# Inverting the delta rule's 64-row blocks: eight tiles in one pass, with the small blocks turned on the engines

## The chip, the cores and the metric

The kernel runs on one core of a Trainium2 chip. A core has five engines that run beside each other, each in the order of its own instructions: TensorE (PE in the profile; its weight loads, which overlap the matmuls, are PEld), VectorE (DVE), ScalarE (ACT), GpSimd (POOL) and SyncE (SP), which in this kernel issues almost all DMAs. The metric is the device time of one execution in microseconds (us); lower is better.

## What is computed

The reference is one layer of a streaming encoder over 1024 rows of 1024 channels. A combined projection feeds two branches: a gated DeltaNet with 8 heads, and a chunked attention with 16 heads. Both are projected, gated, merged, normalised, and followed by a feed-forward part with a short convolution. The change lies in the DeltaNet, in the solve of its chunked delta rule. Cut to what matters:

```
a_low = where(strict, (k_beta @ k^T) * decay, 0)          # per chunk of 64 rows
sol = triangular_solve(a_low + eye, rhs, lower=True, unit_diagonal=True)
u, w = sol[..., :dv], sol[..., dv:]
qk = where(causal, (q @ k^T) * decay, 0)
def step(state, inp):                                     # over the 16 chunks, in order
    v_new = u_n - w_n @ state
    o_n = (q_n * exp(g_n)) @ state + qk_n @ v_new
    state = state * exp(g_last) + k_dec^T @ v_new
```

The kernel works on tiles of 128 rows, so a head has eight tiles (two chunks of the reference each), and it forms the inverse of the unit lower triangular 128x128 matrix of each tile instead of solving.

## The kernel before, in words

The DeltaNet takes about the span's stretch from 80 to 930 us. A loop over the 8 heads `h` runs these stages, in program order: `stage_solve(h)`, `stage_inverse(h)`, some dense blocks of gates (`some_gates`), `stage_k(h+1)`, `stage_q(h+1)`, two pieces of another product (`mod_rows`), `stage_vz(h+1)`, `stage_chain(h)` and `stage_out(h)`. The order of the instructions on each engine is not the program order: a planner lays them out at build time by priorities and by its own estimate of every duration. `stage_inverse`, `stage_chain` and `stage_out` are put 2000 places ahead in priority, and `stage_k(h+1)` is held behind the last chain step of head `h-1` on each engine. Once laid out, an engine keeps its order: a TensorE instruction whose operand is late stops every later one on TensorE, dense work too.

What the stages around the change do, for one head:

- `stage_k` forms `am`, the eight 128x128 matrices (lines 596 to 605), and sends their 32x32 diagonal blocks through DRAM (`fa_d`, lines 606 to 614), so that `fa` holds each of the 32 blocks (4 blocks times 8 tiles) in a partition of its own.
- `stage_solve` inverts the 32 blocks at once by forward substitution on VectorE: 31 steps of one multiplication (line 670) and one reduction (line 672). A partition of `ft` holds 8 columns of one block's inverse. Then four DMAs write `ft` to DRAM (`ft_d`, line 674), and four more read it back (line 677) as diagonal blocks of the eight 128x128 matrices `dt_`, whose remaining entries were set to zero once.
- `stage_inverse` builds the inverse of the whole matrix from its diagonal blocks, in two groups `g` of four tiles. Each group has four waves of small matmuls on TensorE, all in the one PSUM bank of ring `i`, each followed by copies that the next wave needs: `pxt` (line 694), `py` (lines 706 to 708), `pzz` (line 714) and `pT` (line 720). Line 689 transposes 128x512 of `dt_` into `dd` for each group; lines 696, 697, 709 to 711, 716 and 721 empty the waves, and lines 698 to 703 and 717 fill and clear blocks of `am` on GpSimd.
- `stage_chain` goes through the tiles one after another, with matmuls on `am`, `kd`, `at` and the running state (lines 730 to 754). Its waits are TensorE to VectorE or ScalarE and back.

Dense matmuls of 128x128 by 128x512 (line 284 and, after the DeltaNet's middle, those of the attention, lines 891 and 906) stand between these small ones in TensorE's order. SP's order holds the weight loads (line 185) beside the DMAs of lines 674 and 677. POOL subtracts a rounded copy from each 128x1024 weight block (line 180), which takes 2412 ns in the mean.

Of the kernel before, what the change touches and what calls it, by code (L numbers as in the profile page):

```python
# [9 lines left out]
F32 = mybir.dt.float32  # L10
F32R = mybir.dt.float32r
AF = mybir.ActivationFunctionType
ALU = mybir.AluOpType
# [4 lines left out]
P = 128  # L18
# [3 lines left out]
NT = 8  # L22
# [37 lines left out]
_T, _E0, _E1 = ([f"{n}{i}" for i in range(m)] for n, m in (("T", 4), ("A", 7), ("B", 7)))  # L60


def _at(group, step_, n, first=0):
    return tuple((group, first + step_ * i) for i in range(n))
# [11 lines left out]
    "eg": _at("C", 0, 1, 656), "al": _at("C", 0, 1, 720), "dtb": _at("C", 0, 1, 728),  # L76
    "one": _at("C", 0, 1, 736),

    "tmp": tuple(_T), "dT": _at("G", 0, 1), "fa": _at("G", 0, 1, 1024), "dd": _at("G", 512, 2, 2048),
    "xt": _at("G", 256, 2, 3072), "zd": _at("G", 256, 2, 3584),  # L80
    "ft": _at("F", 256, 2), "pr": _at("F", 256, 2, 512), "gt": _at("GG", 512, 2),
    "vn": _at("V", 128, 3), "sn": _at("V", 128, 3, 384), "jk": _at("V", 0, 1, 768),
    **{n: (_E0[i], _E1[i]) for i, n in enumerate(("y0", "y1", "am", "at", "kd", "vs", "sz"))},
# [57 lines left out]
def hybrid_layer(  # L141
# [7 lines left out]
    PE, DVE, ACT, POOL, SP = nc.tensor, nc.vector, nc.scalar, nc.gpsimd, nc.sync  # L149
# [74 lines left out]
    def nm(s):  # L224
        uid[0] += 1
        return f"{s}_{uid[0]}"
# [7 lines left out]
    turn, groups = {}, {}  # L234
# [26 lines left out]
    def ring(key, shape, dtype=F32):  # L261
        return place(step(key, AT[key]), shape, dtype, key)
# [5 lines left out]
    def mtile(name, tag="m"):  # L268
        return pbank(name, tag)
# [156 lines left out]
    with tc.issue_after(mark0["x"]):  # L426
        o = VO["b_gate"]
# [65 lines left out]
    group("SM", "SM", 184)  # L493
    group("V", "SA", 1024)
    group("GG", "GT", 1024)
    dt_ = ring("dT", [P, NT, P])
    POOL.memset(dt_, 0.0)
    POOL.memset(groups["G"][:, 3072:4096], 0.0)
    B = [slice(32 * i, 32 * i + 32) for i in range(4)]

    def big(name):
# [2 lines left out]
    def flat(t_):  # L504
        return t_.rearrange("p t d -> p (t d)")

    def mbank(name, tag="m"):
        return mtile(nm(name), tag).rearrange("p (t d) -> p t d", t=4)
# [47 lines left out]
    def stage_k(h):  # L556

        c = {}
        gb = c["gb"] = big("gb")
        SP.dma_start(flat(gb),  # L560
                     gcum_d[h:h + 1, :].partition_broadcast(P).rearrange("p o s -> p (o s)"))
        mm = c["mm"] = big("mm")
        DVE.tensor_tensor(mm, gb, gc[:, h, :].unsqueeze(2).to_broadcast([P, NT, P]),
                          ALU.subtract)
        ACT.activation(flat(mm), flat(mm), AF.Abs)
        ACT.activation(flat(mm), flat(mm), AF.Exp, scale=-1.0)
        ACT.activation(flat(gb), flat(gb), AF.Exp)
        egl = c["egl"] = sm("egl")
        DVE.tensor_copy(egl, gb[:, :, P - 1])

        kT = c["kT"] = conv_in(h, 1)
        if h == 0:
            dump("kT", flat(kT))
        kd = c["kd"] = big("kd")
        ss = c["ss"] = sm("ss", 2 * NT)
        for g in range(2):
            pk = mbank("pk")
            for t in range(4):
                PE.transpose(pk[:, t, :], kT[:, 4 * g + t, :], ident)
            for t in range(4):  # L580
                u = 4 * g + t
                sumsq(ss[:, u:u + 1], pk[:, t, :])
            for t in range(4):
                u = 4 * g + t
                DVE.tensor_scalar(kd[:, u, :], pk[:, t, :], mm[:, u, P - 1:P], None, ALU.mult)
        kss = sm("kss")
        DVE.tensor_scalar(kss, ss[:, 0:NT], L2_EPS, None, ALU.add)
        rk = rsq(kss, "k")
        bk = c["bk"] = sm("bk")
        DVE.tensor_tensor(bk, rk, beta[:, h, :], ALU.mult)  # L590
        bkk = sm("bkk")
        DVE.tensor_tensor(bkk, bk, rk, ALU.mult)
        nbe = c["nbe"] = sm("nbe")
        DVE.scalar_tensor_tensor(nbe, bkk, -1.0, eg[:, h, :], ALU.mult, ALU.mult)

        am = c["am"] = big("am")
        for g in range(2):
            pk = mbank("pkk")
            for t in range(4):
                PE.matmul(pk[:, t, :], kT[:, 4 * g + t, :], kT[:, 4 * g + t, :],  # L600
                          start=True, stop=True)
            for t in range(4):
                u = 4 * g + t
                DVE.scalar_tensor_tensor(am[:, u, :], pk[:, t, :], bkk[:, u:u + 1],
                                         mm[:, u, :], ALU.mult, ALU.mult)
        fa_d = scr.tile([4, NT, 32, 32], F32, tag="fa_d", bufs=2, name=nm("fa_d"))
        c["ft_d"] = scr.tile([4, NT, 32, 32], F32, tag="ft_d", bufs=2, name=nm("ft_d"))
        for b in range(4):
            SP.dma_start(fa_d[b].rearrange("t i j -> i t j"),
                         am[32 * b:32 * b + 32, :, 32 * b:32 * b + 32])  # L610
        fa = c["fa"] = ring("fa", [P, 32, 32])
        for q in range(4):
            SP.dma_start(fa[32 * q:32 * q + 32].rearrange("p i j -> p (i j)"),
                         fa_d.rearrange("b t i j -> (b t) (i j)"))
        POOL.memset(fa.rearrange("p i j -> p (i j)")[:, 0:1024:33], -1.0)  # L615
        POOL.memset(am[0:64, :, 64:P], 0.0)
        POOL.tensor_tensor(mm, mm, tri.unsqueeze(1).to_broadcast([P, NT, P]), ALU.mult)
        return c
# [43 lines left out]

    def stage_solve(h, c):

        fa, ft_d = c["fa"], c["ft_d"]
        ft = ring("ft", [P, 8, 32])
        POOL.tensor_copy(ft, tt0)
        for i in range(1, 32):
            pr = ring("pr", [P, 8, 32])
            DVE.tensor_tensor(pr[:, :, 0:i + 1], ft[:, :, 0:i + 1],  # L670
                              fa[:, i:i + 1, 0:i + 1].to_broadcast([P, 8, i + 1]), ALU.mult)
            DVE.tensor_reduce(ft[:, :, i:i + 1], pr[:, :, 0:i + 1], AX.X, ALU.add, negate=True)
        for q in range(4):
            SP.dma_start(ft_d[:, :, 8 * q:8 * q + 8, :].rearrange("b t c j -> (b t) (c j)"),
                         ft[32 * q:32 * q + 32].rearrange("p c j -> p (c j)"))
        for b in range(4):
            SP.dma_start(dt_[32 * b:32 * b + 32, :, 32 * b:32 * b + 32],
                         ft_d[b].rearrange("t c j -> c t j"))

    def stage_inverse(h, c):  # L680


        am = c["am"]
        B0, B1, B2, B3 = B
        lo_, hi_ = slice(0, 64), slice(64, P)
        for g in range(2):
            G = slice(4 * g, 4 * g + 4)
            dd = ring("dd", [P, 4, P])
            DVE.transpose(flat(dd), flat(dt_)[:, 512 * g:512 * g + 512])
            px_ = mbank("pxt", "i")  # L690
            for t in range(4):
                u = 4 * g + t
                for i, j in ((B0, B1), (B2, B3)):
                    PE.matmul(px_[i, t, j], am[:, u, i], dt_[:, u, j], start=True, stop=True)
            xt = ring("xt", [P, 4, 64])
            ACT.activation(xt[B0, :, 0:32], px_[B0, :, B1], AF.Copy, scale=-1.0)
            DVE.tensor_scalar(xt[B2, :, 32:64], px_[B2, :, B3], -1.0, None, ALU.mult)
            for b in (B2, B3):
                POOL.tensor_copy(am[b, G, b], dt_[b, G, b])
            POOL.memset(am[B1, G, B0], 0.0)  # L700
            POOL.memset(am[B3, G, B2], 0.0)
            for b in (B0, B1):
                POOL.tensor_copy(am[b, G, b], dt_[b, G, b])
            py = mbank("py", "i")
            for t in range(4):
                PE.matmul(py[B2, t, B3], dd[:, t, B2], xt[:, t, 32:64], start=True, stop=True)
                PE.matmul(py[B0, t, B1], dd[:, t, B0], xt[:, t, 0:32], start=True, stop=True)
                PE.matmul(py[B1, t, B0], xt[:, t, 0:32], dd[:, t, B0], start=True, stop=True)
            DVE.tensor_copy(am[B2, G, B3], py[B2, :, B3])
            DVE.tensor_copy(dd[B1, :, B0], py[B1, :, B0])  # L710
            ACT.copy(am[B0, G, B1], py[B0, :, B1])
            pz = mbank("pzz", "i")
            for t in range(4):
                PE.matmul(pz[lo_, t, lo_], am[:, 4 * g + t, lo_], am[:, 4 * g + t, hi_], start=True, stop=True)
            zd = ring("zd", [P, 4, 64])
            ACT.activation(zd[lo_], pz[lo_, :, lo_], AF.Copy, scale=-1.0)
            POOL.memset(am[hi_, G, lo_], 0.0)
            pT = mbank("pT", "i")
            for t in range(4):
                PE.matmul(pT[lo_, t, lo_], dd[:, t, lo_], zd[:, t, :], start=True, stop=True)  # L720
            DVE.tensor_copy(am[lo_, G, hi_], pT[lo_, :, lo_])

    def stage_chain(h, c):

# [825 lines left out]
```

## Time and profile before

| | us |
|---|---|
| median of 3 runs | 2217.51 |
| lowest and highest of the 3 | 2213.31, 2221.87 |
| the profiled execution | 2222.63 |
| its span, first to last instruction | 2220.5 |

A row of the profile that groups instructions reads: line, engine, operation, result and operands by their names, out and in shapes, the count; then the busy time in us, the mean ns of one, and the idle time of that engine just before them with what ended it. A row of waits reads: who waited for whom, the sum in us, how many times, the longest. A row of windows gives a stretch, its length, and the busy time of PE, PEld, DVE, ACT and POOL in it with their instruction counts in brackets, then the TensorE clock that was granted as a share of full speed, the DMA share and GB/s. A row of the timeline gives the start, the duration, the instruction, and in square brackets the idle time before it.

### The profile page before, as it was taken

To read this page: it belongs to the slowest core of one execution; us is meant where nothing else is said; L and a number is where in the kernel's file an instruction comes from. 1 tells how busy PE (TensorE), PEld (TensorE's weight loads), DVE (VectorE), ACT (ScalarE), POOL (GpSimd) and SP (SyncE) were. 2 spreads that over 40 slices of the span, in tenths; PEclk is the share of its full clock that TensorE was granted. 3 is DMA by queue.
4 is the path that set the end of the run, shared out by engine and by line. 5 is a ranking of instruction groups with operands and counts; after the bars stand their busy time and mean duration, and the time that the engine had idled before them with its cause. 6 is when DMAs were issued, how large, how long until landed. Compare 5 with 4: busy or idle time off the path is not lost.

```text
span 2220.5 us, 31618 instructions
## 1 busy us (share of the span) xinstructions
PE 2140.7 (96%) x11577; PEld 1793.2 (81%) x11577; DVE 1477.9 (67%) x3096; ACT 999.6 (45%) x2127; POOL 500.9 (23%) x495
## 2 busy tenths in 40 slices
PE   7989999999999999999999899999999999999998
PEld 6778788777878787798989788888788888888886
DVE  6478476674758754567776653456998788875754
ACT  5634243443524334566765642234654444453331
POOL 0223233222323322233432422400120000000000
PEclk9999999999999999999999999999999999999999
DMA  9242323323243403211211424332232222275540
GB/s 289 86 121 71 113 80 106 110 74 110 78 120 87 128 24 99 68 51 50 72 55 60 148 96 128 114 128 95 76 102 70 78 83 86 90 260 210 171 152 38
DMA packets 227453, 232.01 MB, mean 104 GB/s; under 512 B 28058, under 2 KB 179027, under 8 KB 227299
## 3 DMA queue, kind: packets, MB, share of 16 engines
q1 hardware_dynamic: 227219, 229.98, 33.0%
q8 instruction: 91, 1.49, 0.3%
q14 instruction: 63, 0.52, 0.1%
q10 hardware_dynamic: 80, 0.03, 0.0%
HBM read 189.02 MB, written 47.23 MB: 106 GB/s over the span
## 4 chain that ended last, share of the span: by engine, by line
PE 49%; DVE 3%; ACT 1%; issue 1%; DMA 0%; POOL 0%; DVEq 0%; SPq 0%; ACTq 0%; POOLq 0%
PE pup L1268 17%; PE pdn L1422 11%; PE pbr L1049 8%; PE pwo L1110 4%; PE pqk L891 2%; PE pv L906 2%; PE po L981 2%; PE pp L966 1%; PE ps L940 1%; PE pn L1133 0%; DMA raw<-in_w_branch_a_dram 0%; DVE G L1329 0%; DVE t L170 0%; DVE kl L1011 0%; DVE pl L970 0%
## 5 line engine op out<-in xcount | busy, mean ns | idle before, releaser
L180 POOL TENSOR_TENSOR wl<-raw,wh 128x1024 fp32r<-128x1024 f32 x85 | 204.8, 2412 | 334.2 <-ACT wh L177 306.3
L1268 PE MATMUL pup<-hh,wop 128*128 128x512 f32 x704 | 224.2, 390 | 0.4 <-ACT G L1305 0.4
L1268 PE MATMUL pup<-t,wop 128*128 128x512 f32 x792 | 189.5, 392 | 1.4 <-DVE cc L1309 0.8
L1268 PEld LDWEIGHTS pup<-t,wop 128*128 128x128 f32 x792 | 148.6, 188 | 34.8 <-DVE cc L1309 1.2
L1422 PE MATMUL pdn<-dop,dop 128*128 128x512 f32 x696 | 161.6, 391 | 0.0
L177 ACT CAST wh<-raw 128x1024 fp32r<-128x1024 f32 x88 | 92.4, 1050 | 147.4 <-DMA raw<-in_w_in_dram 63.8
L1268 PEld LDWEIGHTS pup<-hh,wop 128*128 128x128 f32 x704 | 132.1, 188 | 29.1 <-ACT G L1305 0.8
L1422 PEld LDWEIGHTS pdn<-dop,dop 128*128 128x128 f32 x696 | 130.7, 188 | 28.3
L284 PE MATMUL pqkv<-hh,wh 128*128 128x512 f32 x352 | 142.8, 406 | 0.0
L284 PE MATMUL pqkv<-hl,wh 128*128 128x512 f32 x352 | 140.5, 399 | 0.0
L284 PE MATMUL pqkv<-hh,wl 128*128 128x512 f32 x352 | 140.2, 399 | 0.0
L1268 PE MATMUL pup<-hl,wop 128*128 128x512 f32 x352 | 137.2, 390 | 0.0
L670 DVE TENSOR_TENSOR FT<-FT,G 128x16 f32<-128x16 f32 (+30 forms) x248 | 121.6, 490 | 20.5 <-POOL G L615 13.1
L1310 POOL TENSOR_TENSOR cc<-cc,G 128x512 f32<-128x512 f32 x22 | 44.4, 2019 | 375.5 <-DVE G L1292 352.3
L951 POOL TENSOR_SCALAR G<-G,FT 128x640 f32<-128x640 f32 (+4 forms) x103 | 70.3, 685 | 182.4 <-DVE FT L950 161.6
L177 ACT CAST wop<-wr 128x512 fp32r<-128x512 f32 x104 | 61.9, 620 | 99.4 <-DVE wr L1250 66.9
L284 PE MATMUL pgt<-hh,wh 128*128 128x512 f32 x240 | 95.6, 399 | 0.4 <-DVE tmp L537 0.4
L284 PE MATMUL pgt<-hh,wl 128*128 128x512 f32 x240 | 94.7, 395 | 0.0
L284 PE MATMUL pgt<-hl,wh 128*128 128x512 f32 x240 | 94.7, 395 | 0.0
L180 DVE TENSOR_TENSOR wop<-wr,wop 128x512 fp32r<-128x512 f32 x104 | 75.3, 731 | 16.8 <-ACT wop L177 16.2
L970 DVE TENSOR_TENSOR pl<-pp,ph 128x512 fp32r<-128x512 f32 (+2 forms) x116 | 72.5, 635 | 17.4 <-ACT ph L969 16.6
L948 ACT ACTIVATE G<-G,FT 128x640 f32<-128x640 f32 (+4 forms) x103 | 71.6, 695 | 18.9 <-DVE FT L943 16.9
(413 smaller groups left out, 5786.2 us busy)
## 6 DMA issues: line engine op xcount, KB each, us to landing
raw<-in_w_in_dram SPq DMA_DIRECT2D x72, 512.0 KB
wr<-in_w_up_dram SPq DMA_DIRECT2D x44, 512.0 KB
dwr<-in_w_down_dram SPq DMA_DIRECT2D x44, 512.0 KB
raw<-in_w_ada_dram SPq DMA_DIRECT2D x32, 512.0 KB
wa<-in_w_ada_dram SPq DMA_DIRECT2D x32, 256.0 KB
gates_d<-GT SPq DMA_DIRECT2D x32, 256.0 KB
g_d<-G SPq DMA_DIRECT2D x15, 512.0 KB
rel_d<-in_rel_bias_dram SPq DMA_DIRECT2D x16, 383.5 KB
```

The costliest lines, as they stand in the source:

```text
L177: he.copy(h, src)
L180: return le.tensor_tensor(l, src, f(h), ALU.subtract).ins
L284: i = PE.matmul(ps, a[:, k, :], r[k][:, 512 * n:512 * n + 512], start=(k == 0 and a is wh and r is rh), stop=(k == NK - 1 and a is wl))
L670: DVE.tensor_tensor(pr[:, :, 0:i + 1], ft[:, :, 0:i + 1], fa[:, i:i + 1, 0:i + 1].to_broadcast([P, 8, i + 1]), ALU.mult)
L891: PE.matmul(ps, a[:, k, :], r[:, k, 512 * n:512 * n + 512], start=(k == 0 and a is w[0] and r is hh), stop=(k == NK - 1 and a is w[1]))
L948: ACT.activation(sb[:, 0:n], sb[:, 0:n], AF.Exp, bias=mx[:, nb - 1:nb], scale=-1.0, accum_out=mx[:, 2:3])
L951: POOL.tensor_scalar(sb[:, 0:n], sb[:, 0:n], mx[:, 3:4], 0.0, ALU.mult, ALU.add)
L970: DVE.tensor_tensor(pl[:, B, :], pp, f(ph[:, B, :]), ALU.subtract)
L1049: PE.matmul(ps, a[:, k, :], r[k][:, N], start=(k == 0 and a is w[0] and r is rh), stop=(k == NK - 1 and a is w[1]))
L1110: PE.matmul(ps[n], a[:, t, k, :], wo[k][b][:, 512 * n:512 * n + 512], start=(k == 0 and a is mh and b == 0), stop=(k == NK - 1 and a is ml))
L1268: i = PE.matmul(ps, a[:, u, k, :], b[v][k], start=(new and k == 0 and u == 0 and v == 0), stop=(k == 3 and u == 1), skip_group_check=not new)
L1422: PE.matmul(ps[n], self.g[:, u, i * P:i * P + P], self.w[v][:, 512 * n:512 * n + 512], start=(first and u == 0 and v == 0), stop=(last and ...
```

## The change

The eight DMAs through DRAM go. In their place VectorE transposes `ft` (into a buffer of the ring `pr`), sixteen small copies of 32x64 elements, eight on VectorE and eight on ScalarE, place its pieces into the diagonal blocks of `dd`, and four VectorE transposes of 32x256 elements turn these blocks into `dt_`. `dd` is filled that way, so the two 128x512 transposes of line 689 go too. `stage_inverse` then runs its four waves once for all eight tiles, with results packed so that a wave fits in the one bank. The number of matmuls and their sizes stay; each copy between waves does the work of two. `dd`, `xt` and `zd` become single buffers for eight tiles in the same memory and are set to zero once, at the start. The diff, without the declarations of buffers:

```diff
@@ setup
-    dt_ = ring("dT", [P, NT, P])
-    POOL.memset(dt_, 0.0)
-    POOL.memset(groups["G"][:, 3072:4096], 0.0)
+    dt_, dd = ring("dT", [P, NT, P]), ring("dd", [P, NT, P])
+    xt, zd = ring("xt", [P, NT, 64]), ring("zd", [P, NT, 64])
+    for z_ in (dt_, dd, xt, zd):
+        POOL.memset(z_, 0.0)
@@ stage_solve
-        for q in range(4):
-            SP.dma_start(ft_d[:, :, 8 * q:8 * q + 8, :].rearrange("b t c j -> (b t) (c j)"),
-                         ft[32 * q:32 * q + 32].rearrange("p c j -> p (c j)"))
-        for b in range(4):
-            SP.dma_start(dt_[32 * b:32 * b + 32, :, 32 * b:32 * b + 32],
-                         ft_d[b].rearrange("t c j -> c t j"))
+        fr = ring("pr", [P, 8, 32])
+        DVE.transpose(fr.rearrange("p c j -> p (c j)"), ft.rearrange("p c j -> p (c j)"))
+        for b in (1, 3, 0, 2):
+            for q in range(4):
+                dst = dd[B[b], :, 32 * b + 8 * q:32 * b + 8 * q + 8]
+                s_ = fr[B[q], :, 8 * b:8 * b + 8].rearrange("p c t -> p t c")
+                if q % 2:
+                    ACT.copy(dst, s_)
+                else:
+                    DVE.tensor_copy(dst, s_)
+        for b in (1, 3, 0, 2):
+            DVE.transpose(dt_[B[b], :, B[b]], dd[B[b], :, B[b]])
@@ stage_inverse: the loop over two groups of four tiles goes
-        for g in range(2):
-            G = slice(4 * g, 4 * g + 4)
-            dd = ring("dd", [P, 4, P])
-            DVE.transpose(flat(dd), flat(dt_)[:, 512 * g:512 * g + 512])
-            px_ = mbank("pxt", "i")
-            for t in range(4):
-                u = 4 * g + t
-                for i, j in ((B0, B1), (B2, B3)):
-                    PE.matmul(px_[i, t, j], am[:, u, i], dt_[:, u, j], start=True, stop=True)
...
+        px_ = ibank("pxt", 64)
+        for u in range(NT):
+            for i, j, o in ((B0, B1, slice(0, 32)), (B2, B3, slice(32, 64))):
+                PE.matmul(px_[i, u, o], am[:, u, i], dt_[:, u, j], start=True, stop=True)
+        ACT.activation(xt[B0, :, 0:32], px_[B0, :, 0:32], AF.Copy, scale=-1.0)
+        DVE.tensor_scalar(xt[B2, :, 32:64], px_[B2, :, 32:64], -1.0, None, ALU.mult)
+        for b in (B2, B3):
+            POOL.tensor_copy(am[b, :, b], dt_[b, :, b])
+        POOL.memset(am[B1, :, B0], 0.0)
+        POOL.memset(am[B3, :, B2], 0.0)
+        for b in (B0, B1):
+            POOL.tensor_copy(am[b, :, b], dt_[b, :, b])
+        py = ibank("py", 32)
+        for u in range(NT):
+            PE.matmul(py[B2, u, :], dd[:, u, B2], xt[:, u, 32:64], start=True, stop=True)
+            PE.matmul(py[B0, u, :], dd[:, u, B0], xt[:, u, 0:32], start=True, stop=True)
+            PE.matmul(py[B1, u, :], xt[:, u, 0:32], dd[:, u, B0], start=True, stop=True)
+        DVE.tensor_copy(am[B2, :, B3], py[B2])
+        DVE.tensor_copy(dd[B1, :, B0], py[B1])
+        ACT.copy(am[B0, :, B1], py[B0])
+        pz = ibank("pzz", 64)
+        for u in range(NT):
+            PE.matmul(pz[lo_, u], am[:, u, lo_], am[:, u, hi_], start=True, stop=True)
+        ACT.activation(zd[lo_], pz[lo_], AF.Copy, scale=-1.0)
+        POOL.memset(am[hi_, :, lo_], 0.0)
+        pT = ibank("pT", 64)
+        for u in range(NT):
+            PE.matmul(pT[lo_, u], dd[:, u, lo_], zd[:, u], start=True, stop=True)
+        DVE.tensor_copy(am[lo_, :, hi_], pT[lo_])
```

More of the change, by code (lines that the diff above doesn't have):

```diff
@@ L77 @@
     "one": _at("C", 0, 1, 736),
-    "tmp": tuple(_T), "dT": _at("G", 0, 1), "fa": _at("G", 0, 1, 1024), "dd": _at("G", 512, 2, 2048),
-    "xt": _at("G", 256, 2, 3072), "zd": _at("G", 256, 2, 3584),
+    "tmp": tuple(_T), "dT": _at("G", 0, 1), "fa": _at("G", 0, 1, 1024), "dd": _at("G", 0, 1, 2048),
+    "xt": _at("G", 0, 1, 3072), "zd": _at("G", 0, 1, 3584),
     "ft": _at("F", 256, 2), "pr": _at("F", 256, 2, 512), "gt": _at("GG", 512, 2),
@@ L606, in stage_k @@
         fa_d = scr.tile([4, NT, 32, 32], F32, tag="fa_d", bufs=2, name=nm("fa_d"))
-        c["ft_d"] = scr.tile([4, NT, 32, 32], F32, tag="ft_d", bufs=2, name=nm("ft_d"))
         for b in range(4):
@@ L663, in stage_solve @@
     def stage_solve(h, c):
-        fa, ft_d = c["fa"], c["ft_d"]
+        fa = c["fa"]
         ft = ring("ft", [P, 8, 32])
@@ L685, in stage_inverse @@
         lo_, hi_ = slice(0, 64), slice(64, P)
-        for g in range(2):
-            G = slice(4 * g, 4 * g + 4)
-            dd = ring("dd", [P, 4, P])
-            DVE.transpose(flat(dd), flat(dt_)[:, 512 * g:512 * g + 512])
-            px_ = mbank("pxt", "i")
-            for t in range(4):
-                u = 4 * g + t
-                for i, j in ((B0, B1), (B2, B3)):
[L694 to L721, printed above, removed]
@@ new lines, in ibank @@
+        def ibank(name, n):
+            return mtile(nm(name), "i")[:, 0:NT * n].rearrange("p (t d) -> p t d", t=NT)
+        px_ = ibank("pxt", 64)
[4 more added lines that the diff above has]
+        DVE.tensor_scalar(xt[B2, :, 32:64], px_[B2, :, 32:64], -1.0, None, ALU.mult)
```

## The prediction

> **What bounds the kernel now.** I read the page first, then the waits of TensorE, then the windows of the DeltaNet's stretch, and last the timeline around the inverse of single heads. The page's first line and its busy line say:
>
> ```profile
> span 2220.5 us, 31618 instructions
> ...
> PE 2140.7 (96%) x11577; PEld 1793.2 (81%) x11577; DVE 1477.9 (67%) x3096; ACT 999.6 (45%) x2127; POOL 500.9 (23%) x495
> ```
>
> TensorE is busy for 2140.7 of the span's 2220.5 us. The change leaves the count and the sizes of the matmuls alone, so it can only win from the 79.8 us in which TensorE idles, from slow stretches of TensorE that count as busy, and from the ends of the waves. A shorter path on another engine wins nothing by itself. So the next view is what TensorE waited for (sum, times, longest):
>
> ```profile
> PE pxt L694 <- DMA G<-ft_d: 14.4, 8, 6.7
> ...
> PE pks L732 <- DVE SA L747: 4.5, 3, 4.2
> ...
> PE pzz L714 <- POOL am L703: 1.6, 1, 1.6
> ```
>
> The longest sum of all, 14.4 us, is the first wave of the inverse waiting for the blocks to come back from DRAM: the very transfer that the change removes. The windows show where that lies, and what follows it:
>
> ```profile
> 80.00:930.00 850.00, 809.66 (x4863) 672.92 (x4862) 550.53 (x1393) 346.59 (x952) 245.86 (x243) 0.99 0.32 92
> 163.00:169.60 6.60, 3.02 (x23) 2.60 (x24) 4.03 (x9) 4.62 (x11) 3.58 (x7) 0.50 0.52 126
> 425.80:429.00 3.20, 3.20 (x10) 2.52 (x9) 3.07 (x7) 0.55 (x3) 0.81 (x3) 0.50 0.85 268
> 787.70:794.30 6.60, 5.91 (x27) 5.91 (x28) 5.81 (x24) 1.31 (x5) 0.00 (x0) 0.50 0.00 0
> 838.90:842.10 3.20, 3.20 (x9) 2.44 (x8) 1.85 (x9) 0.00 (x0) 0.00 (x0) 0.50 0.01 3
> ```
>
> In the DeltaNet's 850 us TensorE is busy for 809.66 and idle for 40.3, a third of which is the 14.4. VectorE is at 550.53 / 850 = 65% and ScalarE at 41%, so both have room. In four short stretches the granted clock is 0.50. Two of them follow the wait in question, as the timeline of head 0 and head 3 shows (start, duration):
>
> ```profile
> 156.10 0.41 DVE L672 TENSOR_REDUCE FT<-FT 128x8 f32<-128x256 f32 x1
> ...
> 158.14 2.00 SPq L674 DMA_DIRECT2D ft_d<-FT  x4
> ...
> 163.59 1.79 SPq L677 DMA_DIRECT2D G<-ft_d  x4
> ...
> 166.54 0.99 PE L694 MATMUL pxt<-G,am 128*32 128x32 f32 x16 [6.68 <-DMA G<-ft_d]
> ...
> 417.95 0.42 DVE L672 TENSOR_REDUCE FT<-FT 128x8 f32<-128x256 f32 x1
> ...
> 424.02 0.25 PE L694 MATMUL pxt<-G,am 128*32 128x32 f32 x2 [2.12 <-DMA G<-ft_d]
> ```
>
> Head 0's solve ends at 156.10 + 0.41 = 156.51; its first wave starts at 166.54, 10.0 us later, and TensorE idles for 6.68 of them. In head 3 the way takes from 418.37 to 424.02, 5.65 us, with 2.12 idle. The stored blocks are read back only 163.59 - 158.14 = 5.45 us after the store is issued, in the same SP queue.
>
> **The change part by part.** *The DMA wait.* 14.4 us go, and the first wave waits for VectorE's last turning transpose instead. How long the turn takes comes from these groups (busy us, mean ns), of VectorE and then of ScalarE, in the stretch 90 to 930:
>
> ```profile
> L689 DVE STREAM_TRANSPOSE G<-G 128x512 f32<-128x512 f32 x16 | 10.4, 691 | 18.8 <-DMA G<-ft_d 18.6
> L670 DVE TENSOR_TENSOR FT<-FT,G 128x184 f32<-128x184 f32 x8 | 10.4, 1296 | 0.2
> ...
> L721 DVE COPY am<-pT 64x256 f32<-64x256 f32 x16 | 6.6, 414 | 14.9 <-PE pT L720 14.7
> ...
> L709 DVE COPY am<-py 32x128 f32<-32x128 f32 x16 | 4.6, 289 | 7.8 <-PE py L708 7.4
> L697 DVE TENSOR_SCALAR G<-pxt 32x128 f32<-32x128 f32 x16 | 4.6, 289 | 3.6 <-ACT G L696 3.2
> ...
> L569 DVE COPY SM<-tmp 128x8 f32<-128x8 f32 x8 | 1.4, 172 | 5.1 <-ACT tmp L567 4.9
> ```
>
> ```profile
> L716 ACT ACTIVATE G<-pzz 64x256 f32<-64x256 f32 x16 | 6.0, 374 | 11.2 <-PE pzz L714 10.9
> ...
> L696 ACT ACTIVATE G<-pxt 32x128 f32<-32x128 f32 x16 | 4.3, 266 | 14.4 <-PE pxt L694 14.3
> L711 ACT COPY am<-py 32x128 f32<-32x128 f32 x16 | 4.0, 252 | 11.0 <-DVE G L710 9.5 <-PE pqkv L284 1.5
> ```
>
> A 256-element transpose lies between half of the 691 ns and all of it; I take 0.42 us, as the 256-element copy's 414 ns. A copy of 64 elements on VectorE lies between the 172 ns of 8 elements and the 289 of 128; I take 0.22. ScalarE's lies at or below the 252 ns of 128 elements; I take 0.25. The turn is one transpose, eight copies on each engine side by side (8 x 0.25 = 2.0 us is the longer), and four transposes: 0.42 + 2.0 + 1.68 = 4.1 us with both engines free, against 5.65 and 10.0 through DRAM. But both engines serve others meanwhile, in a fixed order, so TensorE's place for the first wave can still come too early. Price of that: the waits of TensorE for VectorE and GpSimd above are 4.5 us in 3 and 1.6 in 1, so 0 to 4.2 us for each of the 8 heads, 0 to 33.6 in all. Most hand-overs of the chain do not show in the waits at all, so I take 0.5 each, 4 in all. Net: 14.4 - 4 = 10.4 us won.
>
> *The half clock.* In the 163.00 to 169.60 stretch, TensorE was busy for 3.02 us at 0.50; at the full clock that is half, so 1.5 us go with head 0's wait. The 3.20 us of 425.80 to 429.00 follow head 3's wait and cost 1.6. Together 3.1. The Trainium skill's page "TensorE: Matmul & The Clock Gate", section "HAM oscillation — how this bites in real kernels", warns of idle gaps of TensorE above some 3.4 us; by it head 3's wait of 2.12 us would not lose the clock, and the sum would be 1.6 us smaller. The trace shows 0.50 behind both, so I count both.
>
> *Fewer waves.* A head has four waves where it had eight. What a wave costs besides its matmuls is the pause at its end, here of a `py` wave:
>
> ```profile
> 195.99 0.20 PE L708 MATMUL py<-G 128*32 128x32 f32 x1
> 196.12 0.38 PE L750 MATMUL po<-SA,at 128*128 128x128 f32 x1
> ```
>
> The next matmul starts 0.13 us after the start of the wave's last. I take 0.1 us for each of 4 x 8 = 32 waves saved: 3.2 us (between 0, if other work covers the pause, and 4.2).
>
> *Engine time.* VectorE, per head: added 0.42 + 8 x 0.22 + 4 x 0.42 = 3.9 us; the two transposes of 0.691 go, 1.4; of the wave copies two each of 289, 289, 289 (line 710 taken like 709) and 414 ns (2.56 us) become one each of doubled size, estimated from the 414 ns of 256 elements and the 691 of 512 as 3 x 0.42 + 0.69 = 1.95. Net +1.9 us, 15 over the heads, from 65% to 66.5% of the stretch. ScalarE: 8 x 0.25 added, twice (266 + 252 + 374) become about 0.37 + 0.37 + 0.6: net +1.6, 12.4 over the heads. GpSimd loses instructions. None of these engines is the bound; what hides them is TensorE's dense work. If that cover is gone, at most the 15 us of VectorE show. The turn also stands in VectorE's and ScalarE's queues ahead of chain steps of the head before, for which TensorE waits: a wait like the 4.5 us at line 732 could come from it. I charge 1 us, for the two or three per cent by which the queues grow.
>
> *SP.* Eight issues per head leave SP's queue, in head 0 those of 2.00 and 1.79 us; the second four stand there from the first on until the store has landed, with the weight loads queued behind them. These start earlier now. In TensorE's list the blocks from DRAM lead, no weight does, so I count 0 (a gain of at most those 3.8 us, no loss).
>
> *New order.* The planner lays out the whole stretch anew. Waits like the longest at line 732, 4.2 us, and half-clock stretches like that of 787.70 to 794.30 (5.91 us busy, so 3.0 lost) can come and go with the order. I take 0, with 7 us either way for one such pair.
>
> Sum: -10.4 - 3.1 - 3.2 + 1 = -15.7 us. Against the profiled execution's own 2222.6 that gives 2206.9; that execution stands 5.1 us above the median of 2217.5, from which the same sum gives 2201.8. I forecast 2204, between the two, 0.6% below the median.
>
> **The rivals.** *The wait moves.* The planner puts the first wave where the turn ends by its own estimate, and the turn is as late as the DMAs were, behind other VectorE and ScalarE work. Then the 14.4 and the 3.1 stay, now as waits for VectorE or ScalarE, and 3.2 - 1 is won: 2220.4 by the profiled execution, 2215.3 by the median, about 2217. For it: VectorE's queue is hard to foresee, see the row of line 670, where 184 elements take 1296 ns in the mean while a 512-element transpose takes 691. Against it: the turn's transposes and copies have one source, and the transposes of line 689, also of one source, keep close to 691.
>
> *The turn becomes a longer wait (slower).* The 4.1 us of the turn are stretched by interleaved work of both engines, so that TensorE waits at the first wave of every head, 3.5 us each, and each such wait brings the half clock with 1.6 us lost: 8 x 5.1 = 41 us, against 20.7 won and 1 charged: about +21, 2238. It decides from 20.7 - 1 = 19.7 us in 8 heads on, 2.5 us a head; slower by 11 us needs 3.8 a head. For it: the turn needs thirteen instructions of VectorE in a row and eight answers of ScalarE, where a DMA needs no engine. The Trainium skill's page "VectorE: DVE Perf Modes", section "Rules for kernel authors", speaks the same way: it asks for few instructions, since each in a chain waits for the one before to drain. Against it: thirteen instructions sum to 4.1 us only, and TensorE's list of waits shows 1.6 us in one time as the most that any later wave of the inverse, each fed by such copies, had to wait.
>
> *More than the sum.* If the earlier inverse also clears other idle time of the 40.3 us, a further 10 us: 2194.
>
> **How the numbers follow.** A measurement of this kernel can tell about 0.5%, 11 us, from no change; faster therefore means below 2206.4, slower above 2228.6. The forecast has 0.55, the moved wait 0.28, the longer wait 0.11, more than the sum 0.06. The forecast's own range is 2204 with the 7 us of the order and 5 us for hand-overs: 2194 to 2214; some four fifths of its weight lies on the faster side of 2206.4 once the 2201.8 is counted as likelier than the 2206.9, say 0.42. With the 0.06 of the last case and a little of the second, faster is 0.5. Slower is the third case, 0.11; same is the rest, 0.39. The range for 8 in 10 takes the forecast's low end, a little lowered for the last case, and reaches up through the moved wait: 2192 to 2223.
>
> **What would show it.** In the profile after: no DMA of lines 674 and 677; TensorE's wait for the first wave below 5 us in sum, and for VectorE or ScalarE; from the last reduction to the first wave 4 to 6 us in most heads; no half clock behind it; half as many copies between waves at 1.3 to 1.7 times the time. TensorE's idle time in the stretch near 30 us instead of 40.3. I am wrong if the first wave's waits sum to over 10 us, or if new waits in the chain (lines 732, 736, 742) grow by as much as is won.

## The result and the profile after

The kernel after takes 2239.47 us in the median of 4 runs (2236.21 to 2240.76), the kernel before 2217.9 on the same chip (4 runs). The ratio is 1.0096 [1.0073, 1.0118]: about 21 us slower, where 2204 was forecast and 2223 was the top of the range. The prediction was wrong in sign. In the kernel after, the lines that matter are these: the turn is lines 674 (first transpose), 680 (ScalarE's copies), 682 (VectorE's), 684 (four transposes); the waves are 699, 710 to 712, 718 and 723; `mod_rows` is 826 to 832, the chain 735 to 755. The profiled execution took 2239.85 us. Its page says of the span and the busy times:

```profile
span 2238.1 us, 31574 instructions
...
PE 2144.3 (96%) x11577; PEld 1798.9 (80%) x11577; DVE 1494.7 (67%) x3152; ACT 1017.7 (45%) x2169; POOL 491.1 (22%) x441
```

TensorE idles for 2238.1 - 2144.3 = 93.8 us instead of 79.8, and is busy for 3.6 us more. Both grew, although the transfer it had waited for most is gone. What TensorE waited for, over the whole span:

```profile
PE pks L735 <- DVE SA L750: 11.1, 6, 3.1
PE pk L580 <- ACT y L549: 7.2, 7, 4.8
...
PE py L710 <- DVE G L701: 5.7, 4, 1.4
PE pvn L739 <- DVE SM L544: 5.0, 6, 0.8
...
PE pxt L699 <- DVE G L684: 4.6, 3, 4.0
```

The first wave waits for 4.6 us in sum instead of 14.4, as forecast. But TensorE now waits 11.1 us for the chain's state update (line 750; before 4.5 us), 7.2 for a convolution (before 1.6) and 5.7 for the copy behind the first wave, which before was in no row. (The 5.0 us at line 544, also new, stand in every kernel below that has four waves, the faster ones too, so they don't explain the loss.)

The clock shows the second half of the loss. All stretches at half clock up to the DeltaNet's end, with their sum (columns as before):

```profile
162.50:172.50 10.00, 4.88 (x43) 4.05 (x44) 6.06 (x13) 7.04 (x19) 5.89 (x8) 0.50 0.31 86
220.50:223.70 3.20, 3.20 (x11) 2.81 (x12) 2.42 (x2) 2.80 (x9) 2.29 (x1) 0.50 0.00 0
261.50:271.50 10.00, 8.58 (x25) 6.78 (x26) 1.22 (x4) 1.51 (x8) 0.00 (x0) 0.50 0.00 1
350.20:353.40 3.20, 3.20 (x9) 2.55 (x8) 2.84 (x5) 0.00 (x0) 0.00 (x0) 0.50 0.85 226
445.80:449.00 3.20, 3.18 (x53) 2.74 (x54) 3.09 (x6) 0.00 (x0) 0.00 (x0) 0.50 0.78 203
640.30:646.90 6.60, 5.18 (x59) 4.19 (x59) 5.46 (x10) 0.00 (x0) 0.00 (x0) 0.50 0.85 228
739.30:742.50 3.20, 3.20 (x51) 2.66 (x42) 3.08 (x6) 0.00 (x0) 0.00 (x0) 0.50 0.76 189
930.50:933.70 3.20, 3.20 (x9) 2.50 (x8) 2.31 (x10) 0.00 (x0) 1.26 (x2) 0.50 0.00 0
954.40:957.60 3.20, 3.00 (x15) 2.94 (x15) 2.81 (x10) 2.05 (x6) 0.16 (x1) 0.50 0.00 0
sum 45.80, PE 37.62 PEld 31.23 DVE 29.31 ACT 13.40 POOL 9.61; mean PE 4.18 PEld 3.47 DVE 3.26 ACT 1.49 POOL 1.07
```

TensorE is busy for 37.62 us at 0.50, so 18.8 are lost; before, the four stretches held 3.02 + 3.20 + 5.91 + 3.20 = 15.33, so 7.7 (behind them, from 842 to 1040 us, the clock is 1.00). That is 11.1 us more. With 14.0 us of idle time more and some 6 us less of wave matmuls (their groups are busy for 52.6 us in sum before and 46.5 after), 14.0 + 11.1 - 6 = 19 us, against 2238.1 - 2220.5 = 17.6 between the spans.

The four stretches at 350, 445, 640 and 739 follow the first waves of the inverse of heads 2, 3, 5 and 6. They lose 7.4 of the 18.8 us, and the stretch of head 0, at 162, loses 2.4. The other 9.0 us, at 220, 261, 930 and 954, lie elsewhere; the longest of these, at 261, follows the last steps of head 0's chain, where TensorE has little other work. Head 2 on VectorE shows what happened in the four heads:

```profile
339.02 0.45 DVE L674 STREAM_TRANSPOSE FT<-FT 128x256 f32<-128x256 f32 x1
339.50 1.94 DVE L682 COPY G<-FT 32x64 f32<-32x64 f32 x8
341.47 1.84 DVE L684 STREAM_TRANSPOSE G<-G 32x256 f32<-32x256 f32 x4
345.44 0.49 DVE L826 TENSOR_SCALAR GT<-raw,csil 128x512 f32<-128x512 f32 x1 [2.13 <-issue]
345.96 0.75 DVE L828 SCALAR_TENSOR_TENSOR GT<-raw,csil,GT 128x512 f32<-128x512 f32 x1
346.63 0.34 DVE L750 SCALAR_TENSOR_TENSOR SA<-SA,SM,pu 128x128 f32<-128x128 f32 x1
346.89 1.53 DVE L828 SCALAR_TENSOR_TENSOR GT<-raw,csil,GT 128x512 f32<-128x512 f32 x2
348.45 0.42 DVE L701 TENSOR_SCALAR G<-pxt 32x256 f32<-32x256 f32 x1
```

The turn runs without a break, 339.02 to 343.31, 4.3 us. Behind it stands line 826, the first multiplication of `mod_rows`, which writes a buffer of the ring `gt`. This ring has two buffers, and the gates that fill them leave by a DMA (line 809). VectorE stands still for 2.13 us before line 826, and only behind it come the state update (line 750) and the copy out of the first wave (line 701). TensorE in the same stretch:

```profile
341.89 0.38 PE L745 MATMUL pu<-SA,kd 128*128 128x128 f32 x2
...
342.42 0.70 PE L699 MATMUL pxt<-G,am 128*32 128x32 f32 x32
...
347.03 0.49 PE L735 MATMUL pks<-SA,y 128*128 128x128 f32 x2 [2.09 <-DVE SA L750]
348.93 0.22 PE L710 MATMUL py<-G 128*32 128x32 f32 x1 [1.42 <-DVE G L701]
```

`pu`, the operand of the state update, was there at 341.89 + 0.38 = 342.27, the first wave at 342.42 + 0.70 = 343.12. The answers were there at 346.63 + 0.34 = 346.97 and 348.45 + 0.42 = 348.87, 4.7 and 5.8 us later, for 0.34 and 0.42 us of work. The profile names no releaser for the 2.13 us (it says issue; in head 6 the wait at the same line, 2.95 us, is put down to the DMA `qk_d<-GT`). SyncE had issued a gate's DMA shortly before:

```profile
343.09 0.32 SPq L809 DMA_DIRECT2D gates_d<-GT  x1
```

That the wait is for such a buffer is read from this issue and from the kernel before, where the same instruction stands next behind the solve, and its wait has a name:

```profile
325.83 0.42 DVE L672 TENSOR_REDUCE FT<-FT 128x8 f32<-128x256 f32 x1
330.22 0.48 DVE L823 TENSOR_SCALAR GT<-raw,csil 128x512 f32<-128x512 f32 x1 [3.96 <-DMA gates_d<-GT]
...
331.41 0.34 DVE L747 SCALAR_TENSOR_TENSOR SA<-SA,SM,pu 128x128 f32<-128x128 f32 x1
332.64 1.31 DVE L689 STREAM_TRANSPOSE G<-G 128x512 f32<-128x512 f32 x2 [0.90 <-DMA G<-ft_d]
```

Before, VectorE waited for even longer there, 3.96 us, but the wait lay inside the time in which the blocks were on their way through DRAM, and TensorE's list shows none of it: the 4.2 us at line 732 are those of another head, at 788 us, where two slow multiplications of the next head's solve (2.33 and 2.00 us, line 670) stand in VectorE's order ahead of the state update. Over the 850 us VectorE waited for 20.4 us at this line before and 10.3 after, in the groups' rows, first of before, then of after:

```profile
L823 DVE TENSOR_SCALAR GT<-raw,csil 128x512 f32<-128x512 f32 x8 | 3.9, 483 | 20.4 <-DMA gates_d<-GT 16.4 <-DMA qk_d<-GT 4.0
```

```profile
L826 DVE TENSOR_SCALAR GT<-raw,csil 128x512 f32<-128x512 f32 x8 | 3.9, 483 | 10.3 <-issue 4.0 <-ACT GT L808 3.2 <-DMA qk_d<-GT 2.9
```

VectorE idles half as long at this line as before, and yet TensorE now pays for it. The turn took the place of the DMAs' latency on VectorE itself: the state update comes behind 4.3 us of turn, what is left of the wait, and the first two instructions of `mod_rows`. TensorE's dense work hides only a part of this: of the 4.7 us, 2.09 are idle time.

### The profile page after: what moved, and what is told of

Read it like the earlier page. It is cut to its first block, busy times and chain, and to the rows that moved or that the text cites. A ratio compares the mean times of both kernels' runs of the same rounds, so it can differ in the third digit from the quotient of the medians.

```text
span 2238.1 us, 31574 instructions
## 1 busy us (share of the span) xinstructions
PE 2144.3 (96%) x11577; PEld 1798.9 (80%) x11577; DVE 1494.7 (67%) x3152; ACT 1017.7 (45%) x2169; POOL 491.1 (22%) x441
## 4 chain that ended last, share of the span: by engine, by line
PE 81%; DVE 10%; ACT 4%; DMA 2%; issue 2%; SPq 1%; POOL 0%; DVEq 0%; ACTq 0%; POOLq 0%
PE pup L1271 17%; PE pdn L1425 11%; PE pqkv L284 8%; PE pbr L1052 8%; PE pgt L284 6%; PE pqk L894 6%; PE pwo L1113 4%; PE pv L909 4%; PE po L984 3%; PE pp L969 2%; PE ps L943 2%; PE pz L284 2%; DVE FT L670 2%; DVE y L538 1%; DVE FT L672 1%
## 5 line engine op out<-in xcount | busy, mean ns | idle before, releaser
L670 DVE TENSOR_TENSOR FT<-FT,G 128x16 f32<-128x16 f32 (+30 forms) x248 | 120.9, 488 | 10.8 <-POOL G L615 3.6
L909 PE MATMUL pv<-wh,hh 128*128 128x256 f32 x256 | 75.9, 296 | 4.4 <-DVE kl L1014 4.3
```

The costliest lines, as they stand in the source:

```text
L670: DVE.tensor_tensor(pr[:, :, 0:i + 1], ft[:, :, 0:i + 1], fa[:, i:i + 1, 0:i + 1].to_broadcast([P, 8, i + 1]), ALU.mult)
L909: PE.matmul(ps[:, 0:256], r[:, k, t * P:t * P + P], a[:, k % 4, :], start=(k == 0 and r is hh and a is wh), stop=(k == NK - 1 and r is hl))
```

## The experiments

The theories, as the expectations name them: A, the pile-up in VectorE's queue behind the turn; B, the waves for eight tiles cost by themselves; C, any new order costs by chance; D, the loss comes early, in heads 0 and 1, with chance for the rest. Ratios are to the kernel before, measured beside each.

**Four waves, blocks through DRAM.** The eight DMAs of lines 674 and 677 and two transposes of 128x512 come back; the inverse keeps its four waves for eight tiles.

```diff
...
-        fr = ring("pr", [P, 8, 32])
-        DVE.transpose(fr.rearrange("p c j -> p (c j)"), ft.rearrange("p c j -> p (c j)"))
...
+        for q in range(4):
+            SP.dma_start(ft_d[:, :, 8 * q:8 * q + 8, :].rearrange("b t c j -> (b t) (c j)"),
+                         ft[32 * q:32 * q + 32].rearrange("p c j -> p (c j)"))
+        for b in range(4):
+            SP.dma_start(dt_[32 * b:32 * b + 32, :, 32 * b:32 * b + 32], ft_d[b].rearrange("t c j -> c t j"))
...
+        for g in range(2):
+            DVE.transpose(flat(dd)[:, 512 * g:512 * g + 512], flat(dt_)[:, 512 * g:512 * g + 512])
```

> The blocks go through DRAM as before, with the two 128x512 transposes, but the inverse runs its four waves for eight tiles at once as after. Theory A (the loss sits in VectorE's queue behind the turn: mod_rows' first multiplication stands there, waits for a gate buffer, and the chain step that TensorE needs stands behind it): with DMAs in place of the turn VectorE has 5 us of latency in which that wait is over, so no such pile-up; 2212 to 2220 us, near before or 3 below, the first wave's waits for DRAM about 14 us again. Theory B (the eight-tile waves themselves cost, since every copy between them must be done for all tiles): slower than before by 10 us or more, 2228 to 2240. Theory C (any new order of the plan costs like this by chance): anywhere from 2210 to 2240, with new waits at other lines.

Measured: 2215.0, ratio 0.9977 [0.9968, 0.9987], faster than before by 2.9 to 7.1 us. B falls: the four waves do not cost, they win. TensorE's rows for the first wave (10.8 us, less than the 14 expected and than the 14.4 before) and for the state update:

```profile
PE pxt L696 <- DMA G<-ft_d: 10.8, 7, 6.5
...
PE pks L732 <- DVE SA L747: 2.4, 3, 1.0
```

**The turn on the engines, eight waves.** The two groups of four tiles come back, with the eight waves of the kernel before on `dd`, `xt` and `zd` of the kernel after; the turn stays.

```diff
+        for g in range(2):
+            G = slice(4 * g, 4 * g + 4)
+            px_ = mbank("pxt", "i")
...
```

> The blocks are turned on VectorE and ScalarE as after, but the inverse runs in two groups of four tiles, eight waves, as before. Theory A: the pile-up behind the turn stays, waits of TensorE for line 747/750 (the state update) of some 8 to 11 us in sum and half-clock stretches behind them; 2230 to 2242 us. Theory B: near before, 2210 to 2220. Theory C: anywhere from 2210 to 2240.

Measured: 2238.8, ratio 1.0083 [1.0066, 1.0100]. The loss stays with the turn. TensorE's waits fit A only in part:

```profile
PE pks L735 <- DVE SA L750: 5.9, 6, 2.1
...
PE py L710 <- DVE G L701: 5.0, 2, 4.5
```

The state update accounts for 5.9 us, where A gave 8 to 11. It stands behind line 826 in heads 2, 3 and 6, and ahead of it in head 5; in head 6 the wait shows at `py` instead (4.48 us). The two kernels split the change: the waves alone -0.23%, the turn alone +0.83%, or 1.0096 / 0.9977 = +1.2% on top of the four waves.

**The running sum in a buffer of its own.** So that line 826 need not wait for a gate, `mod_rows` sums in 512 elements of its own, which `ft` and `pr` give up by becoming single; the same edit on the kernel before is the control.

```diff
-    "ft": _at("F", 256, 2), "pr": _at("F", 256, 2, 512), "gt": _at("GG", 512, 2),
+    "ft": _at("F", 256, 1), "pr": _at("F", 256, 1, 256), "own": _at("F", 0, 1, 512), "gt": _at("GG", 512, 2),
...
-            macc[0] = ring("gt", [P, 512])
+            macc[0] = ring("own", [P, 512])
```

> As after, but the running sum of mod_rows has 512 elements of its own (ft and pr have one buffer each instead of two), so that its first multiplication need not wait for a gate buffer's store to land. Theory A: the waits of TensorE for the state update after the turn (9.8 us in heads 2, 3, 5 and 6) and half or more of the 5.7 us at py go, with the half-clock stretches behind them; 2214 to 2224 us. Theory B: within 4 us of after, 2235 to 2243. Theory C: anywhere, with as much wait at other lines.

> Before with the same buffer of its own for the running sum: a control for what that edit, and the new order that comes with it, does by itself. Theories A and B: VectorE's idle time for gate stores (16.4 us) goes but TensorE did not wait for it; within 5 us of before, 2212 to 2222. Theory C: up to 15 us either way.

Measured: 2249.48, ratio 1.0131 [1.0116, 1.0146], and 2249.92, 1.0131 [1.0116, 1.0147]. The opposite of what A expected of the first, and the control tells that the edit is no clean test: it costs some 30 us by itself. With nothing to wait for, the sum moves up into the solve, here in the control between 307.1 and 341.7, a stretch that held none of it before:

```profile
L825 DVE SCALAR_TENSOR_TENSOR FT<-raw,csil,FT 128x512 f32<-128x512 f32 x4 | 5.1, 1287 | 1.7 <-DMA raw<-in_w_ada_dram 1.7
```

The solve is a chain on VectorE almost without a gap (busy for 27.29 of 29.30 us before), and these 5.1 us, the first multiplication and their waits for weights lengthen it by about as much: 34.4 us (307.17 to 341.59) against 29.2 before (297.04 to 326.25). The edit also leaves `ft` and `pr` one buffer each, and no run separates that from the move. With this edit in both, the kernel with the turn and the one with the DMAs take the same time; this fits A, where the turn costs by what stands behind it, but does not prove it. To take the wait away is not the same as to take away what stands behind it.

**The sum held behind the first wave's copy.** The buffers stay; `mod_rows` of heads 2, 3, 5 and 6 may start on each engine only behind line 701. So the state update and line 701 no longer stand behind line 826.

```diff
-        DVE.tensor_scalar(xt[B2, :, 32:64], px_[B2, :, 32:64], -1.0, None, ALU.mult)
+        c["xt"] = DVE.tensor_scalar(xt[B2, :, 32:64], px_[B2, :, 32:64], -1.0, None, ALU.mult).ins
...
-            mod_rows(i)
+            with tc.issue_after(cs[h]["xt"]) if h in (2, 3, 5, 6) else nullcontext():
+                mod_rows(i)
```

> As after, but in heads 2, 3, 5 and 6 the VectorE part of mod_rows is held behind the copy that follows the inverse's first wave, so that its wait for a gate buffer no longer stands ahead of the chain's state update. Theory A (the pile-up behind the turn is most of the loss): the waits of TensorE for the state update (9.8 us in these heads) and at py (5.7 us) go, and three or four half-clock stretches with them: 2217 to 2227 us. Theory D (the loss comes early, from ScalarE's share of the turn and from the plan of heads 0 and 1, and the rest by chance): 5 us or less below after, 2233 to 2240.

Measured: 2223.69, ratio 1.0012 [0.9998, 1.0026], against 1.0096 [1.0073, 1.0118] of the kernel after: 0.84% of 2218, about 18.6 us, come back. Head 2 on VectorE:

```profile
340.86 1.84 DVE L684 STREAM_TRANSPOSE G<-G 32x256 f32<-32x256 f32 x4
342.73 0.35 DVE L750 SCALAR_TENSOR_TENSOR SA<-SA,SM,pu 128x128 f32<-128x128 f32 x1
343.11 0.42 DVE L701 TENSOR_SCALAR G<-pxt 32x256 f32<-32x256 f32 x1
344.66 0.49 DVE L826 TENSOR_SCALAR GT<-raw,csil 128x512 f32<-128x512 f32 x1 [1.13 <-DMA gates_d<-GT]
```

The turn is as long as it was, and line 826 still waits, now by name for the gate's DMA, but the state update follows the turn's end by 0.03 us instead of 3.32. TensorE's waits:

```profile
PE pk L580 <- ACT y L549: 7.2, 7, 4.8
...
PE pvn L739 <- ACT po L555: 6.4, 4, 2.0
...
PE pxt L699 <- DVE G L684: 4.7, 3, 4.1
...
PE pks L735 <- DVE SA L750: 1.6, 3, 0.9
```

The wait for the state update falls from 11.1 to 1.6 us, and the 5.7 at line 710 are gone. Those for the first wave and the convolution stay: they are head 0's, which was not held. In the four held heads a new wait comes instead, `pvn` for ScalarE (line 739: 1.34, 2.03, 1.02 and 2.00 us), and behind heads 3 and 6 a half-clock stretch remains (3.20 and 6.05 us busy, 4.6 lost). So these heads give back 9.8 + 5.7 - 6.4 + 7.4 - 4.6 = 11.9 of the 18.8 us between the two spans. The stretches at 930 and 954 (3.1 us lost) and a wait of 4.3 us at line 909, at 1061 us, are gone as well; that the hold removed them is not shown.

**The same hold on the kernel before.** Behind line 697 of the first group.

```diff
-            DVE.tensor_scalar(xt[B2, :, 32:64], px_[B2, :, B3], -1.0, None, ALU.mult)
+            i_ = DVE.tensor_scalar(xt[B2, :, 32:64], px_[B2, :, B3], -1.0, None, ALU.mult).ins
+            if g == 0:
+                c["xt"] = i_
...
+            with tc.issue_after(cs[h]["xt"]) if h in (2, 3, 5, 6) else nullcontext():
+                mod_rows(i)
```

> As before, with the same hold on mod_rows in heads 2, 3, 5 and 6 (behind the first group's first wave): a control. Before, the wait for the gate buffer lies in the time that the DMAs take. Theory A: held back, VectorE idles through the DMAs and does this work later; a loss of 0 to 10 us, 2218 to 2230. Theory D: within 5 us of before, 2214 to 2224.

Measured: 2240.6, ratio 1.0097 [1.0068, 1.0126], slower by more than any theory gave it. The hold helps only where the turn is on the engines; it is no improvement in itself. Its trace shows where the work went: VectorE now idles through the DMAs (2.82, 6.20, 5.99 and 6.29 us ahead of line 689 in the four heads), and the sum stands between the inverse's waves, in head 2 from 335.96 to 340.39, ahead of the copies out of `py`. TensorE's list then has 4.7 us at line 716, the `pzz` wave, behind ScalarE (before 1.1), and 5.9 for line 654 (before 2.9). Its 5.9 us for the state update are hardly new: one of them, 4.6, is the wait behind the next head's solve that was 4.2 before. No run tells how much of the 20 us these are and how much the rest of the new order.

**All sixteen copies on VectorE.**

```diff
-                if q % 2:
-                    ACT.copy(dst, s_)
-                else:
-                    DVE.tensor_copy(dst, s_)
+                DVE.tensor_copy(dst, s_)
```

> As after, but all sixteen small copies of the turn on VectorE, none on ScalarE. Theory A: the turn is 1.6 us longer and the pile-up behind it stays or grows: 2236 to 2250 us. Theory D: head 0's wait of 4.01 us at the first wave and of 4.78 us for the convolution's ScalarE step behind the turn's copies shrink, with their half-clock stretch: 2226 to 2235 us.

Measured: 2237.09, ratio 1.0077 [1.0059, 1.0095], as slow as the kernel after within the intervals, above the range that D gave. The turn is longer, 6.1 us in head 2, and line 823, the first of `mod_rows` here, follows it there without a wait; still the state update comes 7.3 us after the turn's start (333.95 to 341.28), as it came 7.6 us after it with the wait. TensorE waits for 15.3 us for the first wave and 9.7 for the state update. So ScalarE's share alone is not what costs the time, and in head 2 the longer turn costs as much as the wait did.

**The sum later in the program.** The two calls of `mod_rows` stand behind `stage_vz`.

```diff
-        for i in (2 * h, 2 * h + 1):
-            mod_rows(i)
         if h + 1 < HA:
             stage_vz(h + 1, cs[h + 1])
+        for i in (2 * h, 2 * h + 1):
+            mod_rows(i)
```

> As after, with the calls of mod_rows moved behind stage_vz in program order, so that the planner takes them later in each head where it has the choice. Theory A: where VectorE's first mod_rows instruction leaves the place behind the turn, TensorE's waits for the state update go: 2215 to 2230 us; if the planner puts it there all the same, no change. Theory D: within 5 us of after, or anywhere by chance.

Measured: 2238.9, ratio 1.0089 [1.0071, 1.0106]: no change. Program order did not move them; in heads 2, 3, 5 and 6 the planner kept line 826 behind the turn, and the row is the old one:

```profile
PE pks L735 <- DVE SA L750: 9.9, 5, 4.2
```

**Head 0 held too.** The kernel with the sum held, with head 0 in the list.

```diff
-            with tc.issue_after(cs[h]["xt"]) if h in (2, 3, 5, 6) else nullcontext():
+            with tc.issue_after(cs[h]["xt"]) if h in (0, 2, 3, 5, 6) else nullcontext():
```

> As the run in which mod_rows is held behind the first wave's copy in heads 2, 3, 5 and 6, with the same hold in head 0 too, where six of its VectorE instructions (some 0.75 us each) stand inside the solve. Theory A, widened (what stands on VectorE ahead of the head's path costs, because TensorE waits for that path): head 0's solve ends 3 to 4 us earlier, its wait at the first wave shrinks from 4.1 us, and the half-clock stretch with it: 4 to 10 us below that run, 2212 to 2220, unless weight blocks wait for the buffers that mod_rows then holds longer. Theory D (chance of the order): within 5 us of it either way, or worse.

Measured: 2215.83, ratio 0.9982 [0.9967, 0.9996], faster than before. In head 0 `mod_rows` had stood inside the solve. Without it the first wave comes 3.6 us earlier; first TensorE in the kernel that holds four heads, then in this one:

```profile
161.69 0.25 PE L699 MATMUL pxt<-G,am 128*32 128x32 f32 x2 [4.09 <-DVE G L684]
...
168.16 1.12 PE L580 MATMUL pk<-ident,y 128*128 128x128 f32 x4 [4.78 <-ACT y L549]
```

```profile
158.10 0.32 PE L699 MATMUL pxt<-G,am 128*32 128x32 f32 x2 [2.99 <-DVE G L684]
```

The 4.78 us for the convolution are gone as well. This is not all that the two orders differ in: the half-clock stretch at 261 (8.57 us busy, 4.3 lost in the kernel that holds four heads) has no counterpart here, the clock is 1.00 from 250 to 280.

**Four waves through DRAM, head 0 held.** Does head 0's hold help the kernel with four waves and the DMAs too?

```diff
...
-            mod_rows(i)
+            with tc.issue_after(cs[h]["xt"]) if h in (0,) else nullcontext():
+                mod_rows(i)
```

> The blocks through DRAM and four waves for eight tiles, with mod_rows held behind the first wave's copy in head 0 alone. Theory A, widened: head 0's solve ends 3 to 4 us earlier, and the 6.5 us wait of its first wave for DRAM shrinks to about 3: 2206 to 2213 us, the fastest of all. Theory D: within 5 us of the run without the hold, or worse.

Measured: 2219.21, ratio 0.9998 [0.9988, 1.0007], where 2206 to 2213 was expected: a miss. The first wave's wait in head 0 falls from 6.51 to 2.18 us, but a wait that was not there came behind it:

```profile
158.72 0.25 PE L696 MATMUL pxt<-G,am 128*32 128x32 f32 x2 [2.18 <-DMA G<-ft_d]
164.63 1.11 PE L580 MATMUL pk<-ident,y 128*128 128x128 f32 x4 [3.96 <-ACT y L549]
```

So a part of C holds: a new order can move some 5 us here, and 20 us in the kernel before with the hold, without any change of the work.

**Eight waves, sum held.** The kernel with the turn on the engines and eight waves, with the hold of heads 2, 3, 5 and 6 behind the first group's line that corresponds to 701.

```diff
-            DVE.tensor_scalar(xt[B2, G, 32:64], px_[B2, :, B3], -1.0, None, ALU.mult)
+            i_ = DVE.tensor_scalar(xt[B2, G, 32:64], px_[B2, :, B3], -1.0, None, ALU.mult).ins
+            if g == 0:
+                c["xt"] = i_
...
-            mod_rows(i)
+            with tc.issue_after(cs[h]["xt"]) if h in (2, 3, 5, 6) else nullcontext():
+                mod_rows(i)
```

> The engine turn with two groups and eight waves, and mod_rows held behind the first group's first copy in heads 2, 3, 5 and 6: the turn alone, without the order that piled up behind it. Theory A: 10 to 18 us below the same kernel without the hold (2238.8), so 2221 to 2229, a few us above before: what is left is the turn's own price in heads 0 and 1. Theory D: 2230 to 2242.

Measured: 2221.88, ratio 1.0010 [0.9994, 1.0025], against 1.0083 without the hold: 0.7% come back, as A expected, in another layout of the waves. TensorE's rows:

```profile
PE pT L725 <- ACT G L721: 5.9, 4, 2.4
...
PE pks L737 <- DVE SA L752: 2.3, 3, 0.9
```

The wait for the state update falls from 5.9 to 2.3 us and the 5.0 at `py` are gone; here too a new wait comes, 5.9 us at `pT`. That the hold works in two kernels with different orders, and by nearly the same amount, speaks against C as the cause of the loss. So does the whole series: four kernels with the turn and without the hold, each in an order of its own (the buffer edit aside), lie at 1.0077 to 1.0096, and the two with the hold of four heads at 1.0010 and 1.0012.

## Why the prediction was wrong

*The DMA wait: right.* 14.4 us went and 4.6 came, where 4 were taken, though nearly all of it in head 0 (4.0) and not half a microsecond in each head. The turn takes 4.3 us in head 2, estimated at 4.1. VectorE's copies and transposes were sized well, ScalarE's copies were not (0.25 us taken, 303 ns measured):

```profile
L682 DVE COPY G<-FT 32x64 f32<-32x64 f32 x64 | 14.0, 220 | 1.5
L684 DVE STREAM_TRANSPOSE G<-G 32x256 f32<-32x256 f32 x32 | 14.0, 436 | 2.0 <-ACT G L680 1.2
```

```profile
L680 ACT COPY G<-FT 32x64 f32<-32x64 f32 x64 | 19.4, 303 | 32.8 <-DVE FT L674 31.7
```

*Fewer waves: right, as far as it was measured.* The first experiment wins 2.9 to 7.1 us, and the 3.2 that were forecast lie in that range; but its first wave also waits for 3.6 us less than before, so a part of the win may be the order's. The pause at a wave's end was not measured by itself.

*Engine time: the step that failed.* It counted the turn as 1.9 us more of VectorE per head, hidden by "TensorE's dense work", and charged 1 us for its place ahead of the chain. The price of a place in a fixed order is not its length alone. What stands in front of the chain's state update is the turn, a wait of 1.8 to 3.2 us for a gate buffer and 1.2 us of `mod_rows`, and this wait was in the trace of before, 16.4 + 4.0 us of it, hidden by the very DMAs that the change takes out. The prediction saw the row at line 732 and even said that "a wait like the 4.5 us at line 732 could come from it", but did not list what VectorE's queue held between the last reduction and the state update, nor what released it. In heads 2, 3, 5 and 6 TensorE now waits for 2.09, 3.12, 1.79 and 2.81 us there, 9.8 in sum, and for 5.7 at the copy behind the first wave. (Of the 4.5 us at line 732 that it named, 4.2 had another cause, the slow multiplications at 788 us; but the kind of cost is the same, a place in VectorE's order.)

*The half clock: wrong in sign.* 3.1 us were to be won. The two stretches counted were to go with their waits; but each of the four pile-ups is followed by a stretch, 3.20 + 3.18 + 5.18 + 3.20 = 14.76 us busy, 7.4 lost, head 0's stretch became 10 us long, and four others lose 9.0. In all 11.1 us more were lost. With 9.8 + 5.7 the four heads' pile-ups make 22.9 us. Their hold gave back about 18.6, but 11.9 of it in these heads.

*New order: taken as 0 with 7 us either way.* What is new in head 0 belongs to this term: ScalarE's eight copies (2.49 us, from 161.39 on) stand ahead of the convolution, for which TensorE waits 4.78 us. `mod_rows` stood inside head 0's solve before as well (from 150.78 on). Holding it there won a further 0.3% (0.9982 against 1.0012). The half-clock stretch at 261 and the wait of 4.3 us at line 909 are changes of the order too.

*The rivals.* "The turn becomes a longer wait" gave 2238 and 2239.47 was measured, with a chance of 0.11; yet its place was wrong, and that the number was met is luck. It put 3.5 us at the first wave of every head, where the sum is 4.6 in all; the wait sits behind the turn, at the state update, in four heads. The sign of being wrong that it gave, "new waits in the chain (lines 732, 736, 742) grow by as much as is won", is what came true: these three waits, each for the same instruction as before, grew by 6.6, 3.6 and 0.9 us, and 9.8 were won at the first wave.

*What stays open:* how much of the 20 us that the hold costs on the kernel before the moved work explains, what brought the half-clock stretches at 261, 930 and 954, and how much of the last 5 us either way is the planner's order rather than the work. The kernel after with the sum held in five heads (0.9982) and the four waves with the DMAs left in place (0.9977) both beat the kernel before; they can't be told apart.

## What to carry to other kernels

A transfer that an engine does not take part in is a cover for every wait in that engine's queue at the same time; before taking it out, list what stands in the in-order queue between the transfer's ends, what each entry waits for, and who waits for the entries behind it. Idle time of an engine off the critical path, here 20.4 us of VectorE at one line, costs nothing only as long as that cover lasts. When work is moved onto a busy engine, look at the work that then stands behind a wait, and order that wait last: here one such hold brought back 0.8%, and the same hold cost 1% where the DMAs still covered the wait, while the edit that took the wait away let the work slip ahead into the solve and made things worse.

## What the runs showed of the hardware

Half-clock stretches came behind short gaps: in head 2 after, TensorE idled for 2.09 and 1.42 us within 4.0 us (ended at 347.03 and 348.93), and the granted clock was 0.50 from 350.2 on. In the last steps of head 0's chain three gaps of 0.41, 0.54 and 0.35 us, ended at 258.58, 259.60 and 260.42, stand ahead of the stretch from 261.5 on. But in the kernel before a gap of 2.43 us in head 4, ended at 522.73, was followed by a clock of 1.00 up to 540. The Trainium skill's page "TensorE: Matmul & The Clock Gate", section "HAM oscillation — how this bites in real kernels", gives gaps of more than about 3.4 us; here no gap ahead of these two stretches was that long (2.09 the longest), so the trace differs from the rule as one on single gaps; it does not show what is counted instead.

ScalarE's copy of 32x64 elements took 303 ns, more than its 252 ns for 32x128 out of PSUM before; fewer elements did not make it shorter. The source of the first is cut out of rows at a stride; no run separates this from the memory it lies in.

VectorE's turn nearly keeps its durations (copies 203 to 325 ns, 220 in the mean of 64; transposes 432 to 442 ns, 436 in the mean of 32), while the solve's multiplication with two sources does not: over 8 heads in the kernel after the 128x176 one of line 670 took 342 ns in the mean, the 128x160 one 1653 ns. No run here was made to find the cause of this.
